# Fewer transfers for keys, outputs and gates, a mask inside a running product, and one more tile turned by memory, in a two-mixer transformer layer

## The chip, the core and the metric

The kernel runs on one core of a Trainium2 chip. The core has five engines, each with its own queue of instructions that is worked off in order: TensorE (PE: matmuls, with a separate row for its weight loads, PEld), VectorE (DVE), ScalarE (ACT), GpSimd (POOL) and SyncE (SP), which here issues every transfer (DMA) between the chip's memory (HBM) and the on-chip memory (SBUF). Matmuls write to eight banks of PSUM, each 128 partitions by 512 numbers. Semaphores order the engines among each other. The metric is the time of one execution on the device in microseconds (us); lower is better.

## What is computed

One layer of a streaming encoder, for a prompt of 1024 rows and a sample of 32 rows with a cache of 512; the model width is 1024, all in 32-bit numbers:

```
hn = rmsnorm(h, g_pre)
[qA kA vA gA qB kB vB gB] = hn @ w_in              # eight blocks of 512 columns
oA = band attention, 8 heads of 64: softmax(qA kA / 8 + bias), own 64-row chunk and 8 before it
oB = stick-breaking attention, 8 heads of 64, strictly causal:
     z = qB kB / 8
     w[q, k] = sigmoid(z[q, k]) * prod over k < j < q of sigmoid(-z[q, j])     for k < q, else 0
y  = concat(oA * silu(gA), oB * silu(gB)) @ w_out
h  = h + rmsnorm(y, g_post)
h  = h + sigmoid(h @ w_ple_gate) * (p @ w_ple)
```

The keys and values of both mixers are outputs as well. In the reference the product over j is written as the exponential of a reversed cumulative sum; the kernel forms it as a running product from the last key to the first.

## The kernel before

**How it is tiled.** Every 32-bit operand of a product is split into a high part in the matmul's own format and a low part that is the rest. Three matmuls (high times high, high times low, low times high) then stand for one exact product. The input projection is 32 blocks of 128 output columns; each is worked in three pieces of 352 of the 1056 rows and takes 3 x 24 matmuls. Attention goes head by head in pairs of heads (A0, B0, A1, B1, A2, B2, A3, B3), each head over eight tiles of 128 queries. The last two products, with w_out and w_ple_gate, use Strassen-like products of half the size and stand at the end.

**The stages.** Stage 0 loads and normalises the rows, and projects the first pair. Stages 1 to 8 each weave one pair's attention with the next pair's projection ("dense" matmuls), so that TensorE has work while a head's scores pass through the other engines. In stage 8, beside pair B3, the dense work is the eight gates (gA0 to gA3, gB0 to gB3). Stages 9 to 13 are the per-layer embedding and the last two products.

**The order is a planner's.** Nothing is emitted as it is called. `Recorder` (`rec`, which stands in for the engines as `nc`) notes each operation with what it reads and writes; `order()` simulates all engines with a cost model (`cost`, and the constants `SEM`, `MARGIN`, `ISSUE`, `DMA_START` and others) forwards and backwards for `PASSES` rounds and gives each operation a due time. In the last round ten times its shift is added, from the tables `AHEAD_OF` (by engine and kind) and `AHEAD_AT` (by stage as well). The operations are then emitted in the simulated order. This also decides which PSUM bank a tile gets: all tiles of the pool `ps` share the eight banks, with a least number for each tag in `BANKS`.

**A head's keys.** `prep_k` (and `first_head` for the very first head) makes two operands of 128 partitions by 1024 keys: `kd` holds the high part of a head's 64 dimensions twice, `kl` the low part twice. The engine writes one half; the other half is a copy by transfer from one half to the other. The query operand `L` holds the high part in one half and the low part in the other, so that the two matmuls `L x kd` and `L x kl` in `scores` sum all four partial products.

**Scores and weights of B.** `scores(i)` has 128 (i + 1) keys, in two pieces from tile 4 on. `maskb`, with -1e30 at and above the diagonal, is added to the diagonal block in the bank. Then come sigmoid(-z) into `w0`, sigmoid(z) into `w1`, and the running product in place along `w0` from the right, whose second operand (the bank of scores) is bypassed. GpSimd multiplies the two.

**Turning the weights.** `weights_t(i)` needs each 128 x 128 block transposed. Tiles not named in `ROUND` are turned by TensorE (`ptw`, four blocks to a bank), and ScalarE and VectorE split the bank's content into `wTh` and `wTl`. Tiles in `ROUND` (5, 6, 7 of A; 4, 5, 6 of B) are turned by memory: VectorE transposes squares of 32, one transfer writes them to a scratch in HBM, four transfers fetch them in another order, and the split then reads from SBUF.

**Outputs and gates.** `values(g)` multiplies the weights of four tiles with the values; its two halves of 256 columns each are added in `ot` and stored to `o_dr`. In `col_steps` a gate fetches each third (352 columns) of `o_dr`, multiplies it (for A first by the reciprocal row sums `over`), and stores each third to `og_dr`.

**Sample heads.** `sample_attention` does four heads of the sample at a time; `newest` holds its new weights and values, padded with zeros to 128 partitions.

Of the kernel before, what the change touches and what calls it, by code (L numbers as in the profile page):

```python
# [8 lines left out]
F32 = mybir.dt.float32  # L9
# [19 lines left out]
    ('ACT', ''): -892, ('ACT', 'Kh'): 1659, ('ACT', 'L'): -618, ('ACT', 'S'): 4784,  # L29
    ('ACT', 'hnh'): -1920, ('ACT', 'junk'): -268, ('ACT', 'oT'): -448, ('ACT', 'ot'): 28,  # L30
    ('ACT', 'ple'): 2845, ('ACT', 'sg'): -1594, ('ACT', 'stq'): -1482, ('ACT', 'stv'): -538,
    ('ACT', 'v'): -1004, ('ACT', 'w'): -930, ('ACT', 'wTh'): -102, ('ACT', 'wh'): 77,
    ('ACT', 'whs'): -820, ('ACT', 'wl'): 1080, ('ACT', 'x'): 197, ('ACT', 'xS'): 296,
    ('DVE', 'Kl'): 372, ('DVE', 'L'): 463, ('DVE', 'S'): 119, ('DVE', 'Vh'): 150, ('DVE', 'diags'): 779,
    ('DVE', 'gT'): 1765, ('DVE', 'hnl'): -306, ('DVE', 'kt'): 429, ('DVE', 'newl'): -3638,
    ('DVE', 'om'): 70, ('DVE', 'ot'): -144, ('DVE', 'sgg'): 656, ('DVE', 'sq'): -493,
    ('DVE', 'uu'): 7524, ('DVE', 'w'): -311, ('DVE', 'wTl'): 124, ('DVE', 'wl'): 2196,
    ('DVE', 'wlS'): 2470, ('PE', 'Ss'): -1954, ('PE', 'g'): -930, ('PE', 'mm'): -15, ('PE', 'o'): 149,
    ('PE', 'ple'): 168, ('PE', 'ptr'): 300, ('PE', 'ptws'): 284, ('POOL', 'Qfs'): -48,
    ('POOL', 'be'): -510, ('POOL', 'bias'): -1045, ('POOL', 'g'): 1675, ('POOL', 'gT'): -1894,  # L40
    ('POOL', 'h'): 149, ('POOL', 'ms'): 607, ('POOL', 'ogg'): 81, ('POOL', 'om'): -110,
    ('POOL', 'qsS'): 1220, ('POOL', 'sgg'): 1405, ('POOL', 'w'): -451, ('POOL', 'wl'): -35,
# [3 lines left out]
}  # L46
AHEAD_AT = {
    (0, 'ACT', 'hnh'): 1395, (0, 'ACT', 'stk'): -1192, (0, 'DVE', 'hnl'): 39, (0, 'DVE', 'x'): -1474,
# [6 lines left out]
    (3, 'ACT', 'ot'): -358, (3, 'ACT', 'v'): -1119, (3, 'ACT', 'wh'): 513, (3, 'DVE', 'Kcs'): 45,  # L55
    (3, 'DVE', 'L'): -818, (3, 'DVE', 'Vh'): 157, (3, 'DVE', 'wTl'): -53, (3, 'PE', 'PVl'): 160,
    (3, 'PE', 'S'): 6, (3, 'PE', 'mm'): 89, (3, 'PE', 'ptr'): -5169, (3, 'PE', 'ptws'): 24,
    (3, 'SP', 'be'): 288, (3, 'SP', 'kl'): -604, (3, 'SP', 'swap'): 411, (3, 'SP', 'vns'): 907,
    (4, 'ACT', 'be'): -1790, (4, 'ACT', 'ot'): 139, (4, 'ACT', 'v'): 1170, (4, 'ACT', 'wTh'): 174,
    (4, 'DVE', 'Kcs'): 47, (4, 'DVE', 'Kl'): -350, (4, 'DVE', 'L'): -403, (4, 'DVE', 'Vh'): -176,  # L60
    (4, 'DVE', 'om'): 47, (4, 'DVE', 'vx'): 777, (4, 'DVE', 'w'): 522, (4, 'PE', 'PVs'): -2314,
    (4, 'PE', 'S'): 56, (4, 'PE', 'ptw'): 76, (4, 'SP', 'Kcs'): -1093, (5, 'ACT', 'be'): 42,
    (5, 'ACT', 'stk'): -951, (5, 'ACT', 'wTh'): 150, (5, 'DVE', 'om'): 77, (5, 'DVE', 'ot'): 3568,
# [4 lines left out]
    (6, 'ACT', 'stk'): 1396, (6, 'ACT', 'v'): 2717, (6, 'ACT', 'wTh'): 196, (6, 'ACT', 'wh'): 688,  # L68
    (6, 'DVE', 'S'): 9224, (6, 'DVE', 'om'): 595, (6, 'DVE', 'ot'): 412, (6, 'DVE', 'wTl'): 653,
    (6, 'PE', 'PV'): -108, (6, 'PE', 'PVl'): 183, (6, 'PE', 'S'): 51, (6, 'PE', 'mm'): 186,  # L70
    (6, 'PE', 'ptw'): 112, (6, 'SP', 'g'): 122, (6, 'SP', 'sum'): 227, (6, 'SP', 'wr'): -284,
    (7, 'ACT', 'L'): 381, (7, 'ACT', 'newh'): -334, (7, 'ACT', 'stk'): 3547, (7, 'ACT', 'wTh'): -51,
    (7, 'ACT', 'wh'): -200, (7, 'DVE', 'Vl'): -414, (7, 'DVE', 'diags'): 3279, (7, 'DVE', 'om'): 57,
# [5 lines left out]
    (8, 'ACT', 'wh'): 529, (8, 'DVE', 'S'): 51, (8, 'DVE', 'om'): 721, (8, 'DVE', 'sgg'): 329,  # L79
    (8, 'PE', 'PV'): -75, (8, 'PE', 'S'): 69, (8, 'PE', 'mm'): 310, (8, 'PE', 'ptw'): -55,  # L80
    (8, 'PE', 'ptws'): -1062, (8, 'PE', 'ptxs'): -605, (8, 'POOL', 'Qfs'): -167, (8, 'POOL', 'be'): 856,
    (8, 'POOL', 'ogg'): -399, (8, 'POOL', 'om'): 632, (8, 'POOL', 'sgg'): -2103, (8, 'POOL', 'w'): 1029,
    (8, 'POOL', 'wl'): 261, (8, 'SP', 'Kcs'): 207, (8, 'SP', 'be'): 45, (8, 'SP', 'o'): 668,
    (8, 'SP', 'og'): 832, (8, 'SP', 'ogg'): -634, (8, 'SP', 'swap'): -1099, (9, 'ACT', 'oT'): 3675,
    (9, 'ACT', 'ple'): -989, (9, 'ACT', 'wh'): 1592, (9, 'ACT', 'x'): -1192, (9, 'PE', 'ple'): -270,
# [11 lines left out]
ROUND = {"A": ((5,), (6,), (7,)), "B": ((4,), (5,), (6,))}  # L97
# [143 lines left out]
class Op:  # L241
    __slots__ = ("pieces", "eng", "what", "args", "kw", "key", "busy", "late", "ready", "left", "after", "at", "size", "shared", "table", "start", "shift", "due", "size_", "index", "users", "tiles", "old", "ldw", "kind")
# [3 lines left out]
SEM = 60  # L246
# [4 lines left out]
ISSUE = 480  # L251
# [3 lines left out]
DVE_SET, POOL_SET = 137, 110  # L255


BANKS = {'mm': 1, 'S': 2, 'T': 1, 'PV': 1}
PASSES = 9
# [157 lines left out]
class Recorder:  # L417
# [42 lines left out]
    def node(self, eng, what, args, kw, after):  # L460
        o = Op()
        o.eng, o.what, o.args, o.kw, o.after = eng, what, args, kw, after
        o.key = (self.cls if eng == "PE" else self.low, len(self.ops), len(self.ops))
        o.shared, o.table, o.shift, o.busy, o.late, o.ldw, o.kind = False, None, 0, 0, 0, 0, None
        self.ops.append(o)
        return o

    def add(self, eng, what, args, kw):
# [34 lines left out]
        if eng == "PE":  # L503
            o.ldw = LOAD * args[1].shape[-1]
        if eng == "SP":
            o.pieces = max(self.pieces(v) for v in args[0:2])
# [14 lines left out]
    def cost(eng, method, args, kw, writes, reads):  # L521
# [4 lines left out]
        if eng == "PE":  # L526
            if method == "transpose":
                return 3.5 + 0.4444 * args[1].shape[0], 165
# [3 lines left out]
        if eng == "DVE":  # L532
            if method == "tensor_tensor_scan":
                return 155 + 2.08 * n, 0
# [1772 lines left out]
```

## Time and profile before

| What | Value |
|---|---|
| Runs, us | 767.8, 767.4, 762.78 |
| Median, us | 767.4 |
| Profiled execution, us | 771.36 |
| Its span, first to last instruction, us | 769.5 |
| Mean granted TensorE clock | 0.995 |
| Transfers issued by the kernel's own queue, MB | 172.83 |

The profiled execution is 1.9 us longer than its span and 4.0 us longer than the median of the three runs. In the tables of groups, a row gives the operation, what it writes and reads, its shapes and count; after the first bar the time in which any of them ran and the mean of one in ns; after the second bar the engine's idle time just before them and what ended it. In tables of stretches, a row gives start and end, the length, then busy time and count for PE, PEld, DVE, ACT and POOL, the granted clock, the mean busy share of the 16 DMA engines, and GB/s. In the chain, a row is start, length, and the work. A wait is "who <- whom: us in all, times, longest". All rows carry one source line, that of the emitter, so work is told apart by the names of tiles: `be` stands for all of the heap, `w0` and `w1` of both mixers included.

### The profile page before, as it was taken

Reading aid. Unit: us, or ns where it says so; the run is one execution under the profiler, and the core shown is the slowest. Engines: PE = TensorE matmul, PEld = TensorE weight load, DVE = VectorE, ACT = ScalarE, POOL = GpSimd, SP = SyncE. Lnnn points to the kernel's source line nnn. Section 1 sums busy time; section 2 is a strip of 40 time slices with the busy share of each in tenths; the row PEclk is TensorE's granted clock in tenths of the full one; section 3 lists DMA queues with packets and bytes.
Section 4 is the critical chain, followed back from the end, with each engine's and each line's share of the span. In section 5 each row is a group of like instructions: output and inputs, shape, how many; then the busy total and the mean of one; then the engine's idle time right before and its main releaser. Section 6 shows DMA issues by size and latency. Waiting matters only on the chain.

```text
span 769.5 us, 14227 instructions
## 1 busy us (share of the span) xinstructions
PE 754.2 (98%) x4410; PEld 694.2 (90%) x4410; DVE 608.4 (79%) x1067; ACT 523.7 (68%) x1122; POOL 449.6 (58%) x503
## 2 busy tenths in 40 slices
PE   8999999999999999989999999999999999999997
PEld 6999999999999999989999999989998877888786
DVE  6828879898789898868898699778444788998975
ACT  5737777887676777876778686755237867884561
POOL 5614537783365563556683455889553429699443
PEclk9999999999999999999999999999999999999999
DMA  8746879787897749887879789896679957869555
GB/s 301 240 124 180 256 183 286 199 237 230 206 230 207 203 125 251 225 229 213 250 225 257 192 226 237 253 254 199 204 246 316 293 155 229 284 213 308 203 173 190
DMA packets 202525, 173.73 MB, mean 226 GB/s; under 512 B 67009, under 2 KB 164649, under 8 KB 202450
## 3 DMA queue, kind: packets, MB, share of 16 engines
q1 hardware_dynamic: 202450, 172.83, 77.7%
q8 instruction: 35, 0.57, 0.3%
q14 instruction: 40, 0.33, 0.1%
HBM read 105.72 MB, written 58.91 MB: 214 GB/s over the span
## 4 chain that ended last, share of the span: by engine, by line
PE 87%; DMA 5%; DVE 2%; ACT 2%; SPq 2%; issue 1%; POOL 1%; ACTq 0%; DVEq 0%; POOLq 0%
PE mm_vA L806 6%; PE mm_kB L806 6%; PE mm_gB L806 6%; PE mm_qA L806 6%; PE mm_qB L806 6%; PE mm_gA L806 6%; PE PVB L806 4%; PE mm_kA L806 4%; PE SA L806 4%; PE ple L806 3%; PE mm_vB L806 3%; PE SB L806 3%; PE PVA L806 3%; PE o3P L806 3%; PE o1P L806 3%; PE g1P L806 3%
## 5 line engine op out<-in xcount | busy, mean ns | idle before, releaser
L806 POOL TENSOR_TENSOR be<-be 128x640 f32<-128x640 f32 (+8 forms) x66 | 85.2, 1296 | 55.6 <-DVE be L806 31.6
L806 DVE TENSOR_TENSOR_SCAN be<-be,SB 128x384 f32<-128x384 f32 (+5 forms) x96 | 91.3, 962 | 9.9 <-ACT be L806 6.6
L806 ACT ACTIVATE be<-SB 128x384 f32<-128x384 f32 (+5 forms) x192 | 84.5, 499 | 18.9 <-DVE be L806 7.6
L806 DVE TENSOR_TENSOR wTl<-be,wTh 128x640 fp32r<-128x640 f32 (+2 forms) x48 | 55.5, 1160 | 9.7 <-ACT wTh L806 9.2
L806 ACT ACTIVATE be<-be,statA 128x640 f32<-128x640 f32 (+3 forms) x64 | 44.4, 695 | 9.8 <-DVE statA L806 9.5
L806 DVE STREAM_TRANSPOSE be<-be 128x640 f32<-128x640 f32 (+3 forms) x56 | 47.8, 864 | 1.6 <-ACT be L806 1.4
L806 ACT CAST wTh<-be 128x640 fp32r<-128x640 f32 (+2 forms) x48 | 37.5, 782 | 10.7 <-DMA be<-swapA 7.4
L806 POOL TENSOR_TENSOR gB<-gB,gB 128x256 f32<-128x256 f32 x32 | 26.1, 839 | 29.5 <-DMA gB<-in_w_ple_gate_dram 26.2
L806 DVE CUSTOM_DVE_ANT_0 be<-SA,biasA 128x320 f32<-128x320 f32 (+3 forms) x64 | 30.0, 482 | 4.8 <-PE SA L806 4.3
L806 PE MATMUL SB<-klB,LB 128*128 128x384 f32 (+5 forms) x96 | 33.2, 346 | 0.0
L806 PE MATMUL SB<-kdB,LB 128*128 128x384 f32 (+5 forms) x96 | 33.0, 344 | 0.0
L806 POOL TENSOR_TENSOR oB<-oB,oB 128x256 f32<-128x256 f32 x32 | 26.5, 852 | 10.3 <-issue 5.3
L806 PE MATMUL ptwB<-ident,be 128*128 128x128 f32 x144 | 28.0, 275 | 3.6 <-ACT be L806 2.2
L806 PE MATMUL SA<-kdA,LA 128*128 128x320 f32 (+4 forms) x96 | 30.5, 321 | 0.0
L806 PE MATMUL SA<-klA,LA 128*128 128x320 f32 (+4 forms) x96 | 29.8, 316 | 0.0
L806 DVE TENSOR_TENSOR wTl<-ptwB,wTh 128x512 fp32r<-128x512 f32 (+3 forms) x48 | 25.3, 544 | 4.6 <-PE PVB L806 3.1
L806 POOL TENSOR_TENSOR sggB<-sggB,oggB 128x352 f32<-128x352 f32 x12 | 13.8, 1148 | 23.3 <-DVE sggB L806 23.3
L806 PE MATMUL ptwA<-ident,be 128*128 128x128 f32 x120 | 26.9, 273 | 0.0
L806 PE MATMUL PVB<-wTh,v2B 128*128 128x512 f32 (+2 forms) x96 | 26.1, 345 | 0.3 <-ACT v2B L806 0.3
L806 ACT CAST wTh<-ptwB 128x512 fp32r<-128x512 f32 (+3 forms) x48 | 21.8, 488 | 6.4 <-PE PVB L806 3.9
L806 POOL TENSOR_TENSOR klA<-stkA,kdA 64x1024 fp32r<-64x1024 f32 (+2 forms) x9 | 20.0, 2226 | 9.6 <-ACT kdA L806 9.4
L806 PE MATMUL PVA<-wTh,v2A 128*128 128x128 f32 (+3 forms) x96 | 22.4, 318 | 2.0 <-ACT wTh L806 2.0
(694 smaller groups left out, 2660.2 us busy)
## 6 DMA issues: line engine op xcount, KB each, us to landing
swapA<-be SPq DMA_DIRECT2D x24, 320.0 KB, 4.4
be<-swapA SPq DMA_DIRECT2D x96, 80.0 KB, 2.7
oB<-in_w_out_dram SPq DMA_DIRECT2D x16, 256.0 KB, 4.7
sum_dro<-oB SPq DMA_DIRECT2D x16, 256.0 KB, 3.4
gB<-in_w_ple_gate_dram SPq DMA_DIRECT2D x16, 256.0 KB, 4.2
sum_drg<-gB SPq DMA_DIRECT2D x16, 256.0 KB, 3.6
x<-in_x_prompt_dram SPq DMA_DIRECT2D x16, 256.0 KB, 4.1
h_dr<-h SPq DMA_DIRECT2D x8, 512.0 KB, 4.5
```

The source lines that it names most:

```text
L806: getattr(getattr(tc.nc, o.what[0]), o.what[1])(*args, **kw)
```

## The change

Seven things change. (1) `kd`'s second half is a second ScalarE cast; `kl`'s second half is zeroed once for each of the two buffers and stays zero, so the product of two low parts is left out of the scores. (2) `ot` takes all 512 columns at once: one copy, one addition, one store. (3) A gate fetches its whole row block in its first third and stores it in its last, gA's scaling is one multiplication, and only gB3 goes by thirds as before. (4) B's mask addition goes. A PSUM bank `unit` holds zeros and, in its last 128 columns, the identity; the last piece's running product starts from 0 and adds `unit`, so it is 0 above the diagonal and becomes 1 on it. Other pieces, and the sample's, read `unit` as the bypassed operand. (5) Tile 3 of B is turned by memory. (6) `newest` is a tile of 32 partitions made for each sample group; the start's idle matmuls read `zeros` in its place, and the heap is 96 columns larger. (7) The planner's model has other constants (a semaphore time for each engine, time between dependent instructions of one engine, an early release, one engine at a time on a bank), two more rounds, and all shifts are new.

In transfers: 34 of keys, 32 of outputs and 28 of gates go; 8 heads x 5 = 40 come. The net is 54.

```diff
 AHEAD_OF = {
-    ('ACT', ''): -892, ('ACT', 'Kh'): 1659, ('ACT', 'L'): -618, ('ACT', 'S'): 4784,
...
+    ('ACT', 'Kh'): 847, ('ACT', 'L'): -810, ('ACT', 'Qfs'): 1255, ('ACT', 'be'): 110,
...
-ROUND = {"A": ((5,), (6,), (7,)), "B": ((4,), (5,), (6,))}
+ROUND = {"A": ((5,), (6,), (7,)), "B": ((3,), (4,), (5,), (6,))}
...
-SEM = 60
+SEM = {"PE": 75, "ACT": 35, "DVE": 35, "POOL": 90, "SP": 27, "CTL": 0}
+AGAIN = {"PE": 0, "ACT": 33, "DVE": 60, "POOL": 83}
+EARLY = {"PE": 0, "ACT": 95, "DVE": 80, "POOL": 40}
...
-ISSUE = 480
+ISSUE = 590
...
-BANKS = {'mm': 1, 'S': 2, 'T': 1, 'PV': 1}
-PASSES = 9
+BANKS = {'mm': 1, 'S': 2, 'T': 1, 'PV': 1, 'unit': 1}
+PASSES = 11
...
+                for b in o.banks:
+                    t = max([t] + [x + SEM[e] for other, x in b.seen.items() if other != e])
...
-    heap = Heap(rec, at, "be", 6880)
+    heap = Heap(rec, at, "be", 6976)
...
+    def lower_keys(h):
+
+        if h not in KLD:
+            KLD[h] = opnd[h].tile([P, SEQ], F32R, tag=f"kl{h}", name=f"kl{h}")
+            nc.gpsimd.memset(f(KLD[h][halves(h)[1]]), 0.0)
+        return KLD[h]
+
     def prep_k(nm, h, st):
...
-        kl = opnd[h].tile([P, SEQ], F32R, tag=f"kl{h}", name=f"kl{nm}{h}")
+        kl = lower_keys(h)
         nc.scalar.copy(kd[r], st[r, 0:SEQ])
+        nc.scalar.copy(kd[o], st[r, 0:SEQ])
         nc.gpsimd.tensor_tensor(kl[r], st[r, 0:SEQ], f(kd[r]), ALU.subtract)
-        dma(f(kd[o]), f(kd[r]))
-        dma(f(kl[o]), f(kl[r]))
...
+    IN_PARTS = (("gB", 3),)
...
             if k == "g" and part == 0:
-                box["og"] = at2.tile([P, CH], F32, tag="bias", name=f"og{kind}{p}_{c}", bufs=2)
-                dma(box["og"], o_dr[n][:, cs])
+                if not c or (kind, p) in IN_PARTS:
+                    box["og"] = og = at2.tile([P, T], F32, tag="stg", name=f"og{kind}{p}_{c}", bufs=3)
+                    whole = cs if (kind, p) in IN_PARTS else slice(0, T)
+                    dma(og[:, whole], o_dr[n][:, whole])
+                    if kind == "gA":
+                        nc.gpsimd.tensor_tensor(og[:, whole], og[:, whole], box["over"][:, whole], ALU.mult)
...
-                nc.gpsimd.tensor_tensor(sg, sg, box["og"], ALU.mult)
-                dma(og_dr[n, :, cs], sg)
+                og = box["og"]
+                nc.gpsimd.tensor_tensor(og[:, cs], sg, og[:, cs], ALU.mult)
+                if (kind, p) in IN_PARTS:
+                    dma(og_dr[n, :, cs], og[:, cs])
+                elif c == NCH - 1:
+                    dma(og_dr[n], og)
...
             if ab == "B":
-                a, b, s = pieces[-1]
-                dg = s[:, b - a - P:b - a]
-                nc.vector.tensor_tensor(dg, dg, maskb, ALU.add)
-                nc.gpsimd.memset(w0[:, n:n + 1], 1.0)
+                nc.gpsimd.memset(w0[:, n:n + 1], 0.0)
...
                 for a, b, s in reversed(pieces):
-                    rev = w0[:, a + 1:b + 1][:, ::-1]
-                    nc.vector.tensor_tensor_scan(rev, rev, s, 1.0 if b == n else w0[:, b + 1:b + 2], ALU.mult, ALU.bypass)
+                    last = b == n
+                    rev = w0[:, a + 1:b + 1 - last][:, ::-1]
+                    unit = units[0][:, a + 1 - b + 512:512] if last else units[0][:, 0:b - a]
+                    nc.vector.tensor_tensor_scan(rev, rev, unit[:, ::-1], 0.0 if last else w0[:, b + 1:b + 2], ALU.mult, ALU.add if last else ALU.bypass)
...
-            for x in range(2):
-                c = slice(2 * x * P, (2 * x + 2) * P)
-                ot = at.tile([P, 2 * P], F32, tag="ot", name=f"ot{nm}_{g}_{x}", bufs=3)
-                nc.scalar.copy(ot[r], acc[o, c])
-                rec.behind()
-                nc.vector.tensor_tensor(ot[r], acc[r, c], ot[r], ALU.add)
-                dma(o_dr[sidx(ab, p)][r, (4 * g + 2 * x) * P:(4 * g + 2 * x + 2) * P], ot[r])
+            ot = at.tile([P, 4 * P], F32, tag="ot", name=f"ot{nm}_{g}", bufs=3)
+            nc.scalar.copy(ot[r], acc[o])
+            rec.behind()
+            nc.vector.tensor_tensor(ot[r], acc[r], ot[r], ALU.add)
+            dma(o_dr[sidx(ab, p)][r, 4 * g * P:(4 * g + 4) * P], ot[r])
...
+    units.append(psum("unit", "unit"))
+    nc.vector.memset(units[0], 0.0)
+    nc.vector.tensor_copy(units[0][:, 384:512], ident)
```

More of the change, by code (lines that the diff above doesn't have):

```diff
@@ L35 @@
[L35 to L40, printed above, removed]
@@ L46 @@
+    ('DVE', 'news'): 142, ('DVE', 'o'): -939, ('DVE', 'oT'): -2081, ('DVE', 'sq'): -898,
+    ('DVE', 'w'): 331, ('DVE', 'wTl'): -26, ('DVE', 'wl'): -2838, ('PE', 'PV'): -5, ('PE', 'PVl'): 51,
+    ('PE', 'S'): -3, ('PE', 'Ss'): 12, ('PE', 'mm'): 7, ('PE', 'o'): -848, ('PE', 'ptws'): -36,
+    ('PE', 'ptx'): -23, ('POOL', 'bias'): 574, ('POOL', 'kl'): -1392, ('POOL', 'o'): -923,
[4 rows of a table added]
 }
 AHEAD_AT = {
-    (0, 'ACT', 'hnh'): 1395, (0, 'ACT', 'stk'): -1192, (0, 'DVE', 'hnl'): 39, (0, 'DVE', 'x'): -1474,
[6 rows of a table removed]
@@ L55 @@
[L55 to L60, printed above, removed]
@@ L82 @@
[L82 to L85, printed above, removed]
[7 rows of a table removed]
[3 rows of a table added]
+    (1, 'SP', 'swap'): 1043, (2, 'ACT', 'kd'): -796, (2, 'ACT', 'om'): 57, (2, 'ACT', 'stq'): 426,
@@ L93 @@
+    (2, 'ACT', 'stv'): -553, (2, 'ACT', 'wh'): -314, (2, 'DVE', 'vx'): -235, (2, 'PE', 'PVl'): -89,
+    (2, 'PE', 'mm'): 25, (2, 'PE', 'ptw'): -3, (2, 'POOL', 'o'): 176, (2, 'SP', 'wr'): -421,
+    (3, 'ACT', 'stv'): -962, (3, 'ACT', 'whs'): -1728, (3, 'DVE', 'v'): -2339, (3, 'PE', 'PV'): 36,
[19 rows of a table added]
 }
-ROUND = {"A": ((5,), (6,), (7,)), "B": ((4,), (5,), (6,))}
+ROUND = {"A": ((5,), (6,), (7,)), "B": ((3,), (4,), (5,), (6,))}
 LAG_T = 2
@@ L241 @@
 class Op:
-    __slots__ = ("pieces", "eng", "what", "args", "kw", "key", "busy", "late", "ready", "left", "after", "at", "size", "shared", "table", "start", "shift", "due", "size_", "index", "users", "tiles", "old", "ldw", "kind")
+    __slots__ = ("pieces", "eng", "what", "args", "kw", "key", "busy", "late", "ready", "left", "after", "at", "size", "shared", "table", "start", "shift", "due", "size_", "index", "users", "tiles", "old", "ldw", "kind", "banks", "early")
 LAND = {"PE": 165, "ACT": 0, "DVE": 0, "POOL": 0, "SP": 0, "CTL": 0}
-SEM = 60
+SEM = {"PE": 75, "ACT": 35, "DVE": 35, "POOL": 90, "SP": 27, "CTL": 0}
+AGAIN = {"PE": 0, "ACT": 33, "DVE": 60, "POOL": 83}
+EARLY = {"PE": 0, "ACT": 95, "DVE": 80, "POOL": 40}
 MARGIN = 400
@@ L463, in node @@
         o.key = (self.cls if eng == "PE" else self.low, len(self.ops), len(self.ops))
-        o.shared, o.table, o.shift, o.busy, o.late, o.ldw, o.kind = False, None, 0, 0, 0, 0, None
+        o.shared, o.table, o.shift, o.busy, o.late, o.ldw, o.kind, o.banks, o.early = False, None, 0, 0, 0, 0, None, (), 0
         self.ops.append(o)
@@ L506, in add @@
             o.pieces = max(self.pieces(v) for v in args[0:2])
+        if eng in ("ACT", "DVE"):
+            o.banks = tuple({id(v.buf): v.buf for v in writes + reads if isinstance(v, View) and v.buf.psum}.values())
         o.shared = eng == "POOL"
@@ L616, in latest @@
             if e != "CTL":
-                free[e] = ends[o.index]
+                free[e] = ends[o.index] - o.early
             done += 1
-            sem = 0 if e == "CTL" else SEM + (MARGIN if e == "PE" else 0)
+            sem = SEM[e] + (MARGIN if e == "PE" else 0)
             for a in before[o.index]:
-                if a.eng == e and e != "SP":
-                    lag = a.busy
+                if a.eng == e and e not in ("SP", "CTL"):
+                    lag = a.busy + AGAIN[e]
                 elif a.eng == "CTL":
@@ L776, in simulate @@
                     port = t + o.busy
-                free[e] = t + o.busy
+                free[e] = t + o.busy - o.early
+                for b in o.banks:
+                    b.seen[e] = t + o.busy
                 done = t + o.busy + o.late
-                last = max(last, free[e])
+                last = max(last, t + o.busy)
             if e != "CTL":
-                o.at, o.start = t, free[e] - o.busy
+                o.at, o.start = t, t
             out.append(o)
             for u in o.users:
-                if u.eng == e and e != "SP":
-                    r = t if e == "CTL" else free[e]
+                if u.eng == e and e not in ("SP", "CTL"):
+                    r = t + o.busy + AGAIN[e]
                 else:
-                    r = done + (0 if u.eng == "CTL" else SEM + (MARGIN if u.eng == "PE" else 0))
+                    r = done + SEM[u.eng] + (MARGIN if u.eng == "PE" else 0)
                 come(u, r)
@@ L858, in stream_step @@
     nc.gpsimd.memset(halfp, -0.5)
[L860 removed]
+    maskb = const.tile([NS, NS], F32, tag="maskb", name="maskb")
     nc.gpsimd.memset(maskb, 0.0)
     nc.gpsimd.affine_select(
[L863 removed]
+        out=maskb, in_=maskb, pattern=[[-1, NS]], base=0, channel_multiplier=1,
         compare_op=ALU.is_gt, fill=NEG,
@@ L1367, in attention @@
         return out
-    newest = [at.tile([P, P + 256], F32R, tag=f"new{x}", name=f"new{x}") for x in "hl"]
-    for x, eng in zip(newest, (nc.vector, nc.gpsimd)):
-        eng.memset(f(x), 0.0)
+    zeros = at.tile([P, 2 * P], F32R, tag="ot", name="zeros", bufs=3)
+    nc.vector.memset(f(zeros), 0.0)
     idle = psum("PV", "idle")
     for _ in range(12):
-        nc.tensor.matmul(idle[:, 0:256], newest[0][:, 0:P], newest[0][:, P:P + 256], start=True, stop=True)
+        nc.tensor.matmul(idle[:, 0:256], zeros[:, 0:P], zeros, start=True, stop=True)
     def sample_attention(ab, gi):
```

61 lines of the change are left out of this document (23 added, 38 removed), and 51 rows, old and new, of tables (AHEAD_AT, AHEAD_OF).

## The prediction

> **What bounds the kernel now.** First the page's head and its table of engines: TensorE (PE) is busy nearly throughout, and "busy" is the union of overlapping matmuls, so it must be checked against the pace of the stream.
>
> ```profile
> span 769.5 us, 14227 instructions
> PE 754.2 (98%) x4410; PEld 694.2 (90%) x4410; DVE 608.4 (79%) x1067; ACT 523.7 (68%) x1122; POOL 449.6 (58%) x503
> q1 hardware_dynamic: 202450, 172.83, 77.7%
> ```
>
> The pace stands in the chain of work that ended last: long runs of one product go at 3.88/24 = 0.16 us for 352 columns and 2.75/12 = 0.23 us for 512, so those stretches are full. The other pieces of that chain tell which transfers it passes through.
>
> ```profile
> 42.23 3.88 PE mm_qA L806 x24
> 206.39 3.00 DMA be<-swapA
> 235.16 3.53 DMA be<-swapA
> 336.67 4.27 DMA be<-swapA
> 455.25 6.37 DMA wr_gA<-in_w_in_dram
> 499.63 5.90 DMA vnsB<-vs_drB
> 649.13 2.75 PE o3P L806 x12
> ```
>
> Then the table of stretches says where TensorE is idle (length less busy time), and what clock it was granted:
>
> ```profile
> 200.00:240.00 40.00, 37.91 (x247) 36.17 (x246) 33.24 (x71) 29.59 (x65) 22.98 (x31) 1.00 0.81 194
> 320.00:400.00 80.00, 77.42 (x478) 74.14 (x477) 65.52 (x100) 57.46 (x121) 50.05 (x58) 0.98 0.81 225
> 440.00:520.00 80.00, 77.50 (x498) 74.49 (x497) 66.72 (x116) 55.92 (x124) 55.87 (x63) 1.00 0.90 241
> 580.00:720.00 140.00, 140.00 (x614) 111.76 (x613) 112.37 (x165) 102.11 (x212) 89.62 (x90) 1.00 0.81 261
> 342.00:343.00 1.00, 0.70 (x3) 0.73 (x4) 1.00 (x3) 0.98 (x3) 0.77 (x1) 0.56 0.58 126
> 343.00:344.00 1.00, 1.00 (x5) 1.00 (x4) 0.97 (x2) 0.36 (x2) 0.45 (x2) 0.50 0.68 165
> 344.00:345.00 1.00, 1.00 (x5) 0.93 (x5) 0.64 (x2) 1.00 (x4) 0.32 (x1) 0.50 0.74 179
> 345.00:346.00 1.00, 1.00 (x6) 0.98 (x6) 0.90 (x3) 0.98 (x3) 0.87 (x2) 0.74 0.87 203
> ```
>
> In the attention stages the idle time is 2.1 + 2.6 + 2.5 = 7.2 us. Behind one of these waits, at 342 us, the granted clock falls to 0.56, 0.50, 0.50 and 0.74 in four successive microseconds: 0.44 + 0.50 + 0.50 + 0.26 = 1.7 us of work lost, without any idle time shown. So 8.9 us of the attention stages is not work. From 580 to 720 us there is none to win. The rest of the idle time (15.3 in all) lies in the first 40 us and the last 10, which the change hardly touches.
>
> Last, who is waited for, and what the queue that issues all transfers (SP) did before one of these waits:
>
> ```profile
> PE ptwB L806 <- ACT be L806: 2.2, 1, 2.2
> PE PVA L806 <- ACT wTh L806: 2.0, 2, 1.3
> PE ptwB L806 <- ACT stvB L806: 1.3, 1, 1.3
> PE ptwsB L806 <- DVE be L806: 1.2, 1, 1.2
> 201.58 1.78 SPq L806 DMA_DIRECT2D klB<-klB  x1
> 204.83 1.99 SPq L806 DMA_DIRECT2D be<-swapA  x4
> ```
>
> The engines named are only the last link. Each of the chain's five transfers above lands at the end of one of these waits or up to 1 us before it: TensorE's next instruction in order needs something that stands in ScalarE's (ACT's) queue behind a tile still in flight. The transfers are late at the source: the four returns behind the wait at 208 us are issued behind a copy of low key halves that alone holds SP for 1.78 us. My reading: TensorE is the bound, and the recoverable part is late transfers.
>
> **The change part by part.** The rows that price it:
>
> ```profile
> L806 PE MATMUL ptwB<-ident,be 128*128 128x128 f32 x144 | 28.0, 275 | 3.6 <-ACT be L806 2.2 <-ACT stvB L806 1.3
> 203.13 0.33 PE ptwA L806 x3
> L806 DVE TENSOR_TENSOR SB<-SB,maskb 128x128 f32<-128x128 f32 x64 | 17.4, 284 | 6.7 <-PE SB L806 5.7 <-ACT otB L806 0.5
> L806 ACT CAST kdB<-stkB 64x1024 fp32r<-64x1024 f32 x8 | 8.4, 1048 | 0.4 <-PE SA L806 0.2
> L806 DVE STREAM_TRANSPOSE be<-be 128x512 f32<-128x512 f32 x8 | 5.6, 699 | 0.0
> L806 DVE TENSOR_TENSOR wTl<-be,wTh 128x640 fp32r<-128x640 f32 x32 | 33.9, 1062 | 7.7 <-ACT wTh L806 7.4
> L806 DVE TENSOR_TENSOR wTl<-ptwB,wTh 128x512 fp32r<-128x512 f32 x24 | 16.2, 680 | 4.1 <-PE PVB L806 3.1 <-ACT wTh L806 1.0
> swapA<-be SPq DMA_DIRECT2D x24, 320.0 KB, 4.4
> swapB<-be SPq DMA_DIRECT2D x8, 320.0 KB, 3.3
> be<-swapB SPq DMA_DIRECT2D x32, 80.0 KB, 2.8
> L806 SPq DMA_DIRECT2D be<-swapB x96: 302/432/1932, 133.3 to 532.2; - x96
> L806 SPq DMA_DIRECT2D o_dr<-otB x32: 445/539/1626, 140.0 to 556.3; - x32
> L806 SPq DMA_DIRECT2D kdB<-kdB x8: 467/483/534, 91.0 to 447.3; - x8
> ```
>
> *Tile 3 of B.* A head of B turns tiles 0, 1, 2, 3 and 7 on TensorE: 1 + 2 + 3 + 4 + 8 = 18 blocks, 144 over eight heads, as the row says. Tile 3 leaves: 8 x 4 = 32 transpositions. Three in a row take 0.33 us of the chain, 0.11 each: 32 x 0.11 = 3.5 us off the bound. Bounds: 0.06 each where the weight load hides behind a matmul (nearest row: 0.16 us for 352 columns, so 128 are 0.06), 1.9; and 28.0/144 = 0.19, 6.2. I take 3.5, since the run of three shows what the queue pays. In return VectorE (DVE) gets 8 x 0.70 = 5.6 us of 32x32 transposing, and its subtractions read memory instead of a bank: 1062 x 512/640 = 850 against 680 ns, 8 x 0.17 = 1.4 us more. SP gets 8 x (1 + 4) = 40 transfers. One round trip is 0.70 + 3.3 + 2.8, plus 2.2 us of issuing (five of 0.43): some 9 us. Its ScalarE copy waits in order, with the next tiles' sigmoids and every copy out of a bank queued behind it. What such waits cost today is bounded by the 48 round trips there are (24 of swapA, 96/4 = 24 of swapB): three of the five waits, 2.2 + 2.0 of idle time and 1.7 of clock, 5.9/48 = 0.12 us each. Eight more: +1.0 (from 0, if the order gives them room, to +7, rival 1).
>
> [...]
>
> *B's mask by the running product.* 64 additions of 284 ns go, 17.4 us of VectorE, and with each a step between scores and sigmoids. The product's second operand is now a fixed bank, with one element less in each tile; its time stays. TensorE never waits for VectorE's mask (no such row among its waits), so 0 here. If anything the bank of scores comes free earlier. Against that, the fixed bank leaves seven of eight for the rotation: no row shows a wait for a bank; 0, bounded by +/-2.6, the idle time of the middle stretch. What hides it: dense projection matmuls, ready to go, stand between the score tiles.
>
> *Keys.* Per head two half-copies by transfer become one more ScalarE cast and a zeroed half written once: 34 transfers of 0.48 or more of SP and some 8 MB fewer; ScalarE gains 16 x 1.05 = 16.8 us of 523.7. Nothing on TensorE. Cover: ScalarE has room at 68%, but one cast is 1 us in its in-order queue ahead of sigmoids; without the cover that is 16 x 1.05.
>
> *Outputs.* Two pieces of 256 columns become one of 512: 32 transfers fewer. VectorE and ScalarE save the fixed part of 32 instructions each. The first half lands later by one piece; its readers are the gates, at 455 us and later: 0.
>
> *Gates.* 48 transfers become 20 and gA's scaling 4 long multiplications instead of 12. The first third of a gate now waits for the whole row block, except in the last gate, kept in pieces. Stretch 580 to 720 shows TensorE full behind them: 0.
>
> *SP together.* 34 x 0.48 + 32 x 0.54 + 28 x 0.43 - 40 x 0.43 = 16.3 + 17.3 + 12.0 - 17.2 = 28 us less issuing, taken from the queue in which the five late transfers stood; bytes fall by 8 less 8 x 0.5 MB = 4 of 172.8. Which of the 8.9 us goes? Copies of keys, pairs of outputs or pieces of gates were issued shortly ahead of these waits. I take two thirds, 5.9; none and all are the ends. What is late next: the same returns, a little less.
>
> *Planner.* All shifts and the model's constants are new, so every engine's order changes. No row prices it: by the nearest rows it can win all 7.2 us of idle time or add as much. I take 0.
>
> Sum: -3.5 + 1.0 - 5.9 = -8.4. The profiled execution lasted 771.36, 1.9 around a span of 769.5, and lies 4.0 above the median of the three runs: 771.4 becomes 763.0, and 767.4 becomes 759.0.
>
> **The rivals.**
>
> 1. *B's first product waits for tile 3* (slower). It is put into the order together with tile 3's turning, and till now had those weights 0.44 us of TensorE later instead of a round trip of 9 us. For: A's last tile is turned in the same way and is the row "PVA <- ACT wTh". Against: dense matmuls can be ordered into the gap. Price: a wait of 2.2 us and its clock loss of 1.7, as at 342 us: 3.9 a head. It decides from 16.1/3.9 = 4.1 heads on, where the time passes 775.1; with five of the eight, 759.0 + 19.5 = 778.5. [...]
>
> 2. *The late transfers stay late.* SP issues fewer, but returns still queue behind what DVE finishes late, and 40 of the new transfers are returns themselves. Then -3.5 + 1.0: 764.9. For: DMA share falls only from 77.7% by about a fortieth. Against: 28 us off SP.
>
> 3. *More goes than is seen as idle.* All 8.9 us, 3.5 of transpositions, and 4 us of pauses too short for an idle row, as VectorE is 17.4 - 5.6 - 1.4 = 10.4 us freer: 767.4 - 16.4 = 751.0. For: B's score chain loses a step 64 times. Against: ScalarE is 16.8 us fuller.
>
> **How the numbers follow.** Chances: forecast 0.45 (own range 755 to 763), rival 1 0.11, rival 2 0.22, rival 3 0.22. About 1% is what a measurement of this kernel can tell from no change: 759.7 and 775.1. Of the forecast six tenths lie below 759.7: faster 0.27 + 0.22 = 0.49; same 0.18 + 0.22 = 0.40; slower 0.11. The range runs from rival 3 to a little beyond rival 2 (its +/-2.6 of the banks and the order): 750 to 769, leaving out rival 1 and the tails.
>
> **What would show it.** Right: 112 ptwB instead of 144; no maskb group; SP's issues fewer by 54; no wait of TensorE over 2 us after 40 us and no granted clock of 0.5 there; idle time of the attention stages near 2 us. Wrong: a row "PVB <- ACT wTh" of several us (rival 1); the same 7 us of idle time under other names (rival 2); or a slower pace than 0.16 us in long runs, which no step of mine foresees.

## The result, and the profile after

| | Before | Changed |
|---|---|---|
| Median, us | 765.59 (8 runs, 762.78 to 767.8) | 760.87 (8 runs, 760.41 to 761.88) |
| Profiled execution's span, us | 769.5 | 759.1 |
| TensorE idle between 40 and 580 us | 7.2 | 1.7 |

The ratio is 0.9942, with a 95% interval from 0.9927 to 0.9956: 0.6% faster, 4.7 us between the medians. That lies inside the stated range and within 1%, the second likeliest of the three outcomes. The changed kernel also scatters less: 1.5 us between its fastest and slowest run against 5.0. Of the runs below, one execution of run 2 (1051.49 us) and one of run 8 (4247.98 us) lie far outside all the others and are left out of the ratios, not of the medians.

The head and the engines on the changed kernel's page:

```profile
span 759.1 us, 13838 instructions
PE 750.3 (99%) x4378; PEld 689.2 (91%) x4378; DVE 606.5 (80%) x981; ACT 534.0 (70%) x1107; POOL 447.5 (59%) x496
q1 hardware_dynamic: 198898, 168.63, 75.9%
```

TensorE has 32 matmuls fewer, ScalarE is 10 us fuller, VectorE all but as full as before, and the queue moved 4.2 MB less. TensorE's waits in the changed kernel (who, for whom, us in all, times, longest):

```profile
PE idle L793 <- DVE zeros L793: 1.2, 1, 1.2
PE ple L793 <- ACT wph1True L793: 0.7, 1, 0.7
PE PVB L793 <- DVE v2B L793: 0.7, 1, 0.7
PE SA L793 <- DVE statA L793: 0.6, 1, 0.6
```

The four waits of the attention stages that the prediction listed are all gone; the longest left there is 0.7 us. The table of stretches, with start and end, length, busy time of the five engines, granted clock, DMA share and GB/s:

```profile
0.00:40.00 40.00, 37.84 (x219) 33.51 (x220) 31.29 (x52) 25.33 (x51) 26.12 (x47) 1.00 0.76 255
40.00:580.00 540.00, 538.29 (x3397) 517.26 (x3396) 434.77 (x719) 391.10 (x820) 313.13 (x346) 1.00 0.78 218
```

540.00 - 538.29 = 1.7 us idle in the attention stages. The clock does not fall anywhere before the last 10 us: a mean of 1.00 over 540 us could hide a short fall, but the mean of this whole execution is 1.000, against 0.995 before. Between the two profiled executions that is 5.5 us of idle time and the 1.7 us of clock at 342 us, beside the transpositions and a second fall of the clock, in the first 12 us (0.90, 0.50 and 0.75 in the three stretches of 2 us from 6 us on), which only the execution before had: there the changed kernel was granted 1.00. These terms do not add up exactly to the 10.4 us between the spans: over the whole span TensorE's idle time falls by 6.5 us (15.3 to 8.8) and its busy time by 3.9 (754.2 to 750.3), less than the prediction's estimate of 3.5 us for the 32 transpositions and the 1.7 us of clock lost in each of the two falls would make together.

### The profile page after: what moved, and what is told of

Same layout as the page of the kernel before. It is cut to its first block, busy times and chain, and to the rows that moved or that the text cites. A ratio compares the mean times of both kernels' runs of the same rounds, so it can differ in the third digit from the quotient of the medians.

```text
span 759.1 us, 13838 instructions
## 1 busy us (share of the span) xinstructions
PE 750.3 (99%) x4378; PEld 689.2 (91%) x4378; DVE 606.5 (80%) x981; ACT 534.0 (70%) x1107; POOL 447.5 (59%) x496
## 4 chain that ended last, share of the span: by engine, by line
PE 94%; DMA 2%; DVE 2%; ACT 1%; SPq 1%; issue 0%; ACTq 0%
PE mm_gB L793 6%; PE mm_kA L793 6%; PE mm_vB L793 6%; PE mm_gA L793 6%; PE mm_qB L793 6%; PE mm_vA L793 6%; PE mm_qA L793 5%; PE mm_kB L793 5%; PE SB L793 4%; PE PVB L793 4%; PE PVA L793 4%; PE SA L793 3%; PE ple L793 3%; PE g1P L793 3%; PE o3P L793 3%; PE o1P L793 3%
## 5 line engine op out<-in xcount | busy, mean ns | idle before, releaser
L793 POOL TENSOR_TENSOR be<-be 128x512 f32<-128x512 f32 (+8 forms) x66 | 86.1, 1313 | 56.5 <-ACT be L793 19.6
L793 DVE TENSOR_TENSOR_SCAN be<-be,unit 128x383 f32<-128x383 f32 (+7 forms) x100 | 93.2, 948 | 17.3 <-ACT be L793 16.2
L793 ACT ACTIVATE be<-SB 128x512 f32<-128x512 f32 (+5 forms) x192 | 83.8, 514 | 17.3 <-PE SB L793 12.6
L793 DVE TENSOR_TENSOR wTl<-be,wTh 128x640 fp32r<-128x640 f32 (+3 forms) x56 | 66.9, 1203 | 5.6 <-ACT wTh L793 5.5
L793 ACT ACTIVATE be<-be,statA 128x640 f32<-128x640 f32 (+2 forms) x64 | 44.6, 698 | 15.3 <-DVE statA L793 11.5
L793 ACT CAST wTh<-be 128x640 fp32r<-128x640 f32 (+3 forms) x56 | 42.3, 762 | 1.8 <-DMA be<-swapB 1.6
L793 DVE CUSTOM_DVE_ANT_0 be<-SA,biasA 128x320 f32<-128x320 f32 (+2 forms) x64 | 30.0, 478 | 7.6 <-PE SA L793 4.0
L793 PE MATMUL SB<-kl,LB 128*128 128x384 f32 (+5 forms) x96 | 33.1, 345 | 0.0
L793 PE MATMUL SA<-kdA,LA 128*128 128x320 f32 (+2 forms) x96 | 30.9, 326 | 0.6 <-DVE statA L793 0.6
L793 PE MATMUL SA<-kl,LA 128*128 128x320 f32 (+2 forms) x96 | 29.8, 314 | 0.0
L793 POOL TENSOR_TENSOR oggB<-sggB,oggB 128x352 f32<-128x352 f32 x12 | 13.4, 1115 | 22.1 <-DVE sggB L793 22.0
L793 DVE TENSOR_TENSOR wTl<-ptwA,wTh 128x128 fp32r<-128x128 f32 (+3 forms) x48 | 22.1, 479 | 3.0 <-ACT wTh L793 2.8
```

Source lines behind the costliest of these rows:

```text
L793: getattr(getattr(tc.nc, o.what[0]), o.what[1])(*args, **kw)
```

## The experiments

Two kinds of run are needed, because a planner makes the order anew for every edit. In some, the order of every engine is kept instruction for instruction and one part is put back in its place. In others the planner's shifts, fitted to one kernel each, are all set to zero, and the order is made anew for each. Differences between two kernels are taken as the difference of their ratios to the kernel before, times 764 us, about the median of its runs beside the experiments (764.1 to 765.0).

**1. Keys by transfer, order kept.** In runs 1 to 3, `instead` names what is emitted in place of an operation, and `also` what is emitted behind it, at the place that the planner gave to that operation. The first head has the same edit.

```diff
         nc.scalar.copy(kd[o], st[r, 0:SEQ])
+        rec.ops[-1].instead = [(("sync", "dma_start"), (f(kd[o]), f(kd[r])), {})]
         nc.gpsimd.tensor_tensor(kl[r], st[r, 0:SEQ], f(kd[r]), ALU.subtract)
+        rec.ops[-1].also = [(("sync", "dma_start"), (f(kl[o]), f(kl[r])), {})]
```

> The changed kernel with every engine's order kept, and the keys' second halves again copied by transfer: 34 transfers come back in SP's queue at the places where ScalarE's second cast and GpSimd's subtraction are emitted, and 17 casts of ScalarE go. Theory T (fewer transfers ended the waits): the copies stand in SP's queue again and part of the 5.9 us returns, 762.5 to 765. Rival O (the new order ended them, and the number of transfers does not matter): 760.1 to 761.7, TensorE's idle time between 40 and 580 us within 1 us of the changed kernel's.

Measured: 782.78 us, ratio 1.0243 (1.0198 to 1.0289). Both theories missed. The longest of TensorE's waits:

```profile
PE mm_vB L795 <- ACT be L795: 4.0, 2, 2.4
PE SA L795 <- DVE wTl L795: 3.4, 2, 2.3
PE SA L795 <- DVE statA L795: 1.6, 1, 1.6
```

An order that counts on a cast of 1.05 us meets a transfer of 3.7 to 4.6 us (medians of the copies of `kd` in this run); TensorE, idle for 1.7 us between 40 and 580 us in the changed kernel, is idle there for 540.00 - 523.49 = 16.5 us in this run. By the ratios the cost is 23 us, and it holds the misfit of an order as well as the price of the transfers; run 10 tells them apart.

**2. Outputs and gates in pieces, order kept.**

```diff
             dma(o_dr[sidx(ab, p)][r, 4 * g * P:(4 * g + 4) * P], ot[r])
+            rec.ops[-1].instead = [(("sync", "dma_start"), (o_dr[sidx(ab, p)][r, (4 * g + 2 * x) * P:(4 * g + 2 * x + 2) * P], ot[r, 2 * x * P:(2 * x + 2) * P]), {}) for x in range(2)]
...
                     dma(og[:, whole], o_dr[n][:, whole])
+                    if (kind, p) not in IN_PARTS:
+                        rec.ops[-1].instead = [(("sync", "dma_start"), (og[:, x * CH:(x + 1) * CH], o_dr[n][:, x * CH:(x + 1) * CH]), {}) for x in range(NCH)]
...
                     dma(og_dr[n], og)
+                    rec.ops[-1].instead = [(("sync", "dma_start"), (og_dr[n, :, x * CH:(x + 1) * CH], og[:, x * CH:(x + 1) * CH]), {}) for x in range(NCH)]
```

> The changed kernel with every engine's order kept, and each output store issued as two transfers, each whole gate load and store as three: 32 + 28 transfers come back, some 26 us of SP's issuing. Theory T: 762.5 to 765, with waits of TensorE behind late returns. Rival O: 760.1 to 761.7.

Measured: 761.69 us, ratio 0.9956 (0.9937 to 0.9976), the changed kernel's within the interval, as rival O had it. The stretch of the attention stages:

```profile
40.00:580.00 540.00, 538.26 (x3397) 516.87 (x3397) 430.29 (x718) 390.21 (x817) 313.41 (x346) 1.00 0.78 218
```

Sixty more transfers in SP's queue, and TensorE is idle for the same 1.7 us. The mere number of these transfers, of outputs and gates, did not make the waits.

**3. The mask's step put back, order kept.**

```diff
                 for a, b, s in pieces:
                     nc.scalar.activation(w0[:, a:b], s, AF.Sigmoid, scale=-1.0)
+                    if b == n:
+                        o = rec.ops[-1]
+                        o.instead = [(("vector", "tensor_scalar"), (dg, dg, 0.0, None, ALU.add), {}), (o.what, o.args, o.kw)]
```

> The changed kernel with every order kept, and 64 VectorE operations of 128 columns on the diagonal block of B's scores put back ahead of the sigmoids (they add zero). Prediction: the mask was worth nothing on TensorE, 760.1 to 761.7. Rival V (VectorE's room and B's shorter chain count): 64 x 0.284 = 18 us of VectorE back, and each of 8 heads pays some 0.3 to 0.6 us, 763 to 766.

Measured: 773.44 us, ratio 1.0107 (1.0079 to 1.0135), 0.0165 or 12.6 us above the changed kernel, where the prediction had nothing and rival V at most 766. In the edit `dg` is the diagonal block of the scores. The groups of B's sigmoids and of the added step (busy, mean ns; idle time before them and what ended it):

```profile
L795 ACT ACTIVATE be<-SB 128x512 f32<-128x512 f32 (+5 forms) x192 | 84.8, 500 | 48.2 <-DVE SB L795 38.8 <-PE SB L795 4.7 <-DMA be<-swapB 3.4
L795 DVE TENSOR_SCALAR SB<-SB 128x128 f32<-128x128 f32 x64 | 17.8, 282 | 5.4 <-PE SB L795 4.8 <-issue 0.2
```

The step costs VectorE 17.8 us, and ScalarE waits 38.8 us for it. One case in this run's order of time (start, length, engine, work, idle time before it):

```profile
113.02 1.22 DVE L795 TENSOR_TENSOR_SCAN be<-be,unit 128x511 f32<-128x511 f32 x1
...
114.15 0.27 DVE L795 TENSOR_SCALAR SB<-SB 128x128 f32<-128x128 f32 x1
114.46 0.44 ACT L795 ACTIVATE be<-SB 128x320 f32<-128x320 f32 x1 [1.23 <-DVE SB L795]
...
115.49 0.30 PE L795 MATMUL ptwB<-ident,be 128*128 128x128 f32 x1 [1.40 <-ACT be L795]
```

The step lasts 0.27 us, but it stands in VectorE's queue behind a running product of 1.22. ScalarE's next instruction waits 1.23 us for it, and TensorE's next in order waits 1.40 for ScalarE. TensorE names ScalarE; VectorE is two links back. Not all of the cost is seen as idle time: of the 12.0 us between the spans of this run and the changed kernel's, 6.2 are idle time of TensorE and 5.8 are longer busy time of the same 4378 matmuls (756.1 against 750.3). And like run 1 this run keeps an order that was planned without the step, so 12.6 us holds some misfit; run 11 plans anew.

**4. Tile 3 on TensorE, order made anew with the changed kernel's shifts.**

```diff
-ROUND = {"A": ((5,), (6,), (7,)), "B": ((3,), (4,), (5,), (6,))}
+ROUND = {"A": ((5,), (6,), (7,)), "B": ((4,), (5,), (6,))}
```

> The changed kernel with tile 3 of B turned by TensorE again; the planner makes a new order with the shifts that were made for the other. Prediction: 32 transpositions of 0.11 us come back, 3.5, less 1.0 for the eight round trips: 763.4. Rival (round trips cost what the transpositions save): 760 to 761.5. Rival O: shifts that do not fit cost several us whatever is turned where, 764 to 770; then the table of TensorE's waits names other pairs than in the changed kernel.

Measured: 779.87 us, ratio 1.018 (1.0144 to 1.0217). The longest wait lies in the last products, where there is no tile 3:

```profile
PE g0P L793 <- ACT junk L793: 3.1, 1, 3.1
```

Rival O of this run had the direction, and its range ended at 770: shifts fitted to another kernel cost far more than the part. The next runs therefore have no shifts.

**5 to 8. No shifts.** Each sets the shift's term to zero; run 7 takes the changed kernel's planner into the kernel before, run 8 has tile 3 on TensorE (the edit of 4).

```diff
-            out, end = self.simulate(lambda o: (0, o.due + last * 10 * o.shift, o.index))
+            out, end = self.simulate(lambda o: (0, o.due + 0, o.index))
```

> The changed kernel with all shifts of the planner at zero: the order is what its model alone gives. Theory O (the order, fitted shift by shift, carries the last per cent): 768 to 785. Theory T (structure carries it): under 764.

> The kernel before with all shifts at zero. Against the run without shifts of the changed kernel it gives what the change is worth where neither order was fitted. Theory T and my sum (8.4 us): 8 us or more above that run. Theory O with a structure worth nothing: within 2 us of it.

> The kernel before with the changed kernel's planner (constants, bank rule, rounds) and no shifts: the new model without the new structure. If the model made the gain, it lies near the changed kernel without shifts (within 3 us); if the structure did, near the kernel before without shifts.

> The changed kernel without shifts, and tile 3 of B on TensorE: tile 3's worth where no order was fitted to either. Prediction: 2.5 us above the changed kernel without shifts (3.5 for 32 transpositions less 1.0 for the round trips). Rival: within 1 us of it or below. A difference over 6 us either way says that the scatter of orders is larger than the term.

| Run | Median, us | Ratio to the kernel before | 95% interval |
|---|---|---|---|
| 5, changed | 765.12 | 1.0010 | 1.0001 to 1.0020 |
| 6, before | 769.96 | 1.0066 | 1.0047 to 1.0086 |
| 7, before, new model | 769.70 | 1.0071 | 1.0052 to 1.0090 |
| 8, changed, tile 3 on TensorE | 769.26 | 1.0061 | 1.0044 to 1.0077 |

Without fitting, the change is worth 0.0056, 4.3 us: the same as with it (0.0058, 4.4). Fitting is worth 5.0 us to the kernel before and 5.2 to the changed one. The new model is worth nothing by itself (6 against 7). So the gain goes with the change's parts and not with its fitted order; it is half of the 8 us that theory T had for run 6, and twice the 2 us of theory O.

Tile 3 is 0.0051, 3.9 us, and the intervals of 5 and 8 do not overlap. The stretches of the attention stages, first of run 5:

```profile
40.00:580.00 540.00, 535.63 (x3379) 513.84 (x3378) 430.84 (x717) 387.14 (x815) 317.23 (x345) 1.00 0.76 216
```

and of run 8:

```profile
40.00:580.00 540.00, 535.67 (x3399) 513.10 (x3399) 431.13 (x712) 387.84 (x814) 315.83 (x345) 1.00 0.74 208
```

The idle time is the same 4.3 to 4.4 us in both. The difference is work that TensorE no longer does: over the whole span it is busy for 751.4 us in run 5 and 755.4 in run 8, 4.0 more. The eight round trips cost no idle time here.

**9 to 12. One part at a time, no shifts.** Run 9 is run 7 with tile 3 by memory and nothing else; its `ROUND` for B is ((3,), (4,), (5,), (6,)). Runs 10 to 12 are run 5 with one part as in the kernel before, planned anew: the keys' transfers (10), the mask added in the bank and the product read from the scores, with the heap as before to make room for the mask (11), outputs in two pieces and gates in three (12). Their diffs are the corresponding lines of the change, taken back.

> The kernel before with the changed kernel's planner, no shifts, and tile 3 of B turned by memory as the only other change. If tile 3 is nearly the whole gain (theory P, TensorE's 32 transpositions): 4 us under the same kernel without it (769.7), 765 to 766.5. If it needs the other parts to pay (theory T: room in SP's queue for its 40 transfers): 768 or more.

> The changed kernel without shifts, keys' second halves by transfer as before, planned anew: 34 transfers come back. Theory P: 764.5 to 766 (the changed kernel without shifts took 765.1). Theory T: 767 or more. The same part undone within a fixed order cost 22 us; if it costs under 1 here, those 22 were the misfit of an order, not the price of the transfers.

> The changed kernel without shifts, B's mask added in the bank as before, planned anew. Prediction: 764.5 to 766. Rival V (64 steps fewer in B's chain count): 767 or more.

> The changed kernel without shifts, outputs in two pieces and gates in three, planned anew: 60 transfers come back. Theory P: 764.5 to 766. Theory T: 767 or more.

| Run | Median, us | Ratio to the kernel before | 95% interval | Against |
|---|---|---|---|---|
| 9, tile 3 alone | 772.28 | 1.0089 | 1.0065 to 1.0113 | run 7: +0.0018, 1.4 us |
| 10, keys back | 767.50 | 1.0038 | 1.0011 to 1.0064 | run 5: +0.0028, 2.1 us |
| 11, mask back | 774.72 | 1.0121 | 1.0089 to 1.0153 | run 5: +0.0111, 8.5 us |
| 12, pieces back | 762.40 | 0.9967 | 0.9953 to 0.9980 | run 5: -0.0043, -3.3 us |

*The mask* costs most when it is taken back. In run 5 the sigmoids hardly wait, and not for VectorE:

```profile
L793 ACT ACTIVATE be<-SB 128x512 f32<-128x512 f32 (+5 forms) x192 | 82.8, 517 | 3.2 <-DMA swapB<-be 1.6 <-PE SB L793 0.8 <-POOL be L793 0.3
```

and in run 11 they wait for the mask (SB) and for the running product (be), which reads the bank of scores again:

```profile
L793 ACT ACTIVATE be<-SB 128x512 f32<-128x512 f32 (+5 forms) x192 | 84.3, 506 | 37.1 <-DVE SB L793 14.2 <-DVE be L793 12.8 <-DVE wTl L793 2.9
```

The waits for these two are 14.2 + 12.8 = 27.0 us, in an order that was planned with the mask in it. In none of the runs 5, 8 and 12 and the changed kernel, which all lack the mask, do ScalarE's sigmoids wait for them. Their idle time as a whole says less: it is 25.2 us in run 8, for other reasons and at little cost. What counts is TensorE, which in run 11 is idle for 540.00 - 527.23 = 12.8 us in the attention stages against 4.4 in run 5, and mostly names other work of VectorE, which stands in the same queue:

```profile
40.00:580.00 540.00, 527.23 (x3314) 502.77 (x3313) 445.60 (x772) 383.39 (x801) 313.53 (x343) 0.99 0.74 210
PE SB L793 <- DVE LB L793: 2.9, 2, 1.5
PE ptwA L793 <- DVE wTl L793: 1.6, 1, 1.6
```

8.4 us more of idle time stand beside 8.5 us more of time.

*Tile 3 alone* gains nothing: the intervals of 9 and 7 overlap, and the difference is on the wrong side. The 32 transpositions are gone, yet TensorE's busy time is 754.0 us against 753.8 in run 7, because the clock fell to 0.50 behind two waits (at 266 and 437 us; by the granted clock of 262 to 270 and 434 to 443 us some 5 us of work were lost; the runs of 9 were granted 0.992 to 0.995 in the mean, those of 7 0.998 to 0.999). TensorE's waits in run 9 show where, and so does the order of time at 262 us:

```profile
PE SB L817 <- DVE be L817: 2.5, 3, 1.2
PE SsA L817 <- ACT QhsA L817: 2.1, 1, 2.1
```

```profile
262.35 0.31 PE L817 MATMUL SB<-klB,LB 128*128 128x320 f32 x1
263.82 0.44 PE L817 MATMUL SB<-kdB,LB 128*128 128x384 f32 x1 [1.17 <-DVE be L817]
264.10 0.34 PE L817 MATMUL SB<-klB,LB 128*128 128x384 f32 x1
265.38 0.44 PE L817 MATMUL SB<-kdB,LB 128*128 128x384 f32 x1 [0.95 <-DVE be L817]
```

New scores wait for a bank that the running product still reads. Tile 3's work on VectorE comes on top of the mask's: ScalarE's waits for the mask rise from 8.2 us in run 7 to 14.2 here. The second fall stands behind waits of the sample's products (SsA), which nothing here ties to tile 3. That tile 3 by memory pays only where the mask's step is gone from VectorE's queue and the bank is free after the sigmoids fits this, and is not shown: room in SP's queue, which theory T of this run named and whose time it met (768 or more), was not tested apart from it.

*Keys*: 2.1 us in the direction of theory T, but the intervals of 10 and 5 overlap, so the time alone does not show a gain. The traces point the same way. In the chain of work that ended last, transfers and their issuing have 3% of the span in run 5, and 15% in run 10 (first run 5, then run 10):

```profile
PE 88%; DVE 5%; DMA 2%; ACT 2%; SPq 1%; issue 1%; POOL 0%; DVEq 0%; ACTq 0%
PE 71%; DMA 11%; DVE 7%; SPq 4%; ACT 3%; issue 2%; POOL 2%; DVEq 0%; ACTq 0%; POOLq 0%
```

ScalarE's casts of the tiles turned by memory wait 8.2 + 6.4 = 14.6 us for the returns of B and A in run 10, and 4.9 in run 5 (first run 5, then run 10):

```profile
L793 ACT CAST wTh<-be 128x640 fp32r<-128x640 f32 (+3 forms) x56 | 42.4, 765 | 5.1 <-DMA be<-swapB 4.9
L793 ACT CAST wTh<-be 128x640 fp32r<-128x640 f32 (+3 forms) x56 | 43.0, 767 | 18.4 <-DMA be<-swapB 8.2
```

In the kernel before this wait is 10.5 us, in the changed one 1.6, in run 1 22.1. It also moves with the order: over all kernels here it is 3.4 to 22.1 us with the keys' copies and 0.7 to 7.4 without them. *Outputs and gates*: undoing them is faster by 3.3 us without shifts, intervals apart, and no different in the fixed order of run 2, where those waits for returns are 1.1 us. They show no gain from fewer transfers. How far two orders that differ by chance lie apart was not measured, so 2 or 3 us cannot be told from such scatter, and 4 us only with care. The parts do not add: 3.9 + 2.1 + 8.5 - 3.3 = 11.2 us for four parts undone singly, against 4.3 for all of them together, so none of them can be called the part of the 4.3 that it made. The mask alone in the kernel before was not tried.

No run was faster than the changed kernel with its shifts. Run 12's structure with shifts fitted to it was not tried.

## Why the prediction was right in direction, and too large

*The bound and what is recoverable: right.* 7.2 us of idle time and one fall of the clock were named; 1.7 us of idle time and no fall are left. All signs that were named for it came: 112 `ptwB`, no group of the mask, 54 issues of SP fewer (918 and 864), no wait over 2 us after 40 us.

*The transpositions: right, a little small.* "3.5 us off the bound" and 1.0 back make 2.5; 3.9 net by runs 5 and 8, at equal idle time. The waits priced from the 48 older round trips did not appear in the changed kernel. In run 9 the eight more saved nothing, so the term needed a condition; which one is open.

*The mask: wrong, and the main failure.* "TensorE never waits for VectorE's mask (no such row among its waits), so 0 here." The row that mattered was not TensorE's. In the profile before, the group of sigmoids already showed 7.6 us behind the running product and 4.6 behind the mask; in the changed kernel both are gone, and what is left is waiting for TensorE's scores (before, then changed):

```profile
L806 ACT ACTIVATE be<-SB 128x384 f32<-128x384 f32 (+5 forms) x192 | 84.5, 499 | 18.9 <-DVE be L806 7.6 <-DVE SB L806 4.6 <-issue 3.2
L793 ACT ACTIVATE be<-SB 128x512 f32<-128x512 f32 (+5 forms) x192 | 83.8, 514 | 17.3 <-PE SB L793 12.6 <-DVE wTl L793 1.3 <-DVE Vl2sB L793 1.3
```

The prediction quoted the mask's own row and not its reader's. Taken back, the mask costs 8.5 us (run 11) or, in a fixed order, 12.6 (run 3). In the case shown under run 3, a step of 0.27 us behind a running product of 1.22 us in VectorE's queue left ScalarE waiting for 1.23 us and TensorE for 1.40. What the mask cost is not room on VectorE as a whole: that engine is busy for 606.5 us after 608.4, where rival 3 had it 10.4 freer, because among others its 32 subtractions of 640 columns from memory grew from 1062 to 1277 ns each.

*The late transfers: the loss was there, the cause holds in part.* The 5.9 us were put down to 28 us of issuing taken off SP. Sixty transfers of outputs and gates put back changed nothing in run 2 and were faster in run 12, so their share of the 28 us was worth nothing here. The keys' 34 are another matter: with them back in run 10, returns are late again (14.6 us of ScalarE's waiting against 4.9), beside 2.1 us of time whose intervals overlap. So the prediction counted issues, and these runs do not bear out the count. How much of the idle time went with the keys and how much with the mask is open. One reading behind the term was also too neat: the five transfers land 0.9, 0.9, 1.1, 1.4 and 2.6 us ahead of the end of the waits, not "up to 1 us".

*Keys, outputs, gates: 0 for their own work on TensorE was near enough*, with the two differences above left open. For the fixed bank, "no row shows a wait for a bank" was a misreading: the row "ptwB <- ACT stvB" is most likely one, since `ptwB` does not read `stvB`, but needs a bank such as ScalarE empties by copying to `stvB`. With seven banks such waits did not grow: that row is gone in the changed kernel.

*The planner: 0 was right.* Fitted shifts are worth 5 us, to both kernels alike.

*The size.* 8.4 us forecast, 4.7 measured. The base explains part of it. The one profiled execution before took 771.36 us, 5.8 above the median of the eight runs, and its idle time and its fall of the clock at 342 us were counted as if every run had them. Its mean clock was 0.995; of the 49 other executions of the kernel before beside the experiments, 48 were granted 0.996 or more and 27 of them 0.999 or more, so most of the clock's loss was not in a usual run. How much of the 7.2 us of idle time was is not known, since no other execution of that kernel has a trace. Between the two profiled spans the difference is 10.4 us, more than forecast. Whether the wrong terms also cancelled is not shown. That the forecast time, 759.0 us, missed by only 1.9 where the gain missed by 3.7 is luck: the median of eight runs before is 1.8 us below that of the first three.

*The rivals.* Rival 1 did not come: no wait of B's products for their weights, and 0.7 us for v2B. Rival 2's gain, 2.5 us, is nearer to the measured 4.7 than the forecast's 8.4, but its sign, the same 7 us of idle time under other names, did not come. Of rival 3, the shorter chain of B counts (run 11) and the freer VectorE did not come; its price was too large.

## What to carry to other kernels

Look for what the waiting engine's releaser waits for, two links back: in run 3 a step of 0.27 us between two other engines was waited for 1.23 us, with a running product of 1.22 us ahead of it in its queue. Where an order is planned and fitted, undoing one part within that order (23 us for the keys, 2.1 when planned anew) prices mostly the misfit; compare versions that are all planned anew and none fitted. And do not take a single profiled execution as the base of a sum when the runs scatter by more than the effect.

## What the runs showed of the hardware

The clock of TensorE fell behind some of the gaps shown here, not behind all. In run 9 two idle stretches of 1.17 and 0.95 us within 3 us were followed by a granted clock of 0.50:

```profile
262.00:266.00 4.00, 1.89 (x9) 0.99 (x7) 3.97 (x7) 3.64 (x10) 3.21 (x4) 0.98 0.92 256
266.00:268.00 2.00, 1.96 (x6) 1.55 (x6) 2.00 (x5) 0.44 (x2) 1.88 (x3) 0.50 1.12 275
```

In the kernel before, one gap of 2.24 us was followed by 0.56 and 0.50 from 342 us on. But in run 1 TensorE was idle for 4.00 - 1.56 = 2.44 us between 344 and 348 us (the longest single wait of that run is 2.4), and the clock stayed at 1.00:

```profile
344.00:348.00 4.00, 1.56 (x10) 1.19 (x9) 3.23 (x6) 3.99 (x10) 0.88 (x3) 1.00 0.71 199
348.00:350.00 2.00, 2.00 (x16) 1.91 (x14) 2.00 (x2) 2.00 (x7) 1.67 (x3) 1.00 0.85 235
```

TensorE was busy for 1.56 of these 4.00 us, less than the 1.89 ahead of the fall in run 9. So of these two cases the one without a fall had the longer idle time and the less busy 4 us; what decides is open. Rival 1 priced a loss of clock behind each wait of 2.2 us: in the kernel before there was one, in run 1 there was none behind 2.44 us, and in run 9 there was one behind 1.17 + 0.95 = 2.1 us.
